# GpSimd takes low weight parts of the mixer's projections, plain float32 leaves, and both ends of the kernel are rearranged

## The chip, the cores and the metric

The kernel runs on one NeuronCore of a Trainium2 chip. TensorE (PE) multiplies matrices, VectorE (DVE), ScalarE (ACT) and GpSimd (POOL) work element by element, SyncE (SP) issues most transfers. The metric is the device time of one execution in microseconds (us). Before the change it is 904.86 us, the median of 3 runs (904.58 to 906.59).

## The reference

The reference is an encoder trunk of two layers on 256 tokens of width 1024, in float32. Each layer adds a mixer and a convolutional feed-forward block to x:

```
h = RMSNorm(x)
p = h @ w_in                       # 1024 -> 16 + 26 * 256 columns
x = x + (sig(gate_dn) * (DeltaNet(q, k, v, beta, g) @ w_dn)
       + sig(gate_hg) * (HGRN2(hq, hf, hb, hi) @ w_hg)) @ w_out
gate, up = RMSNorm(x) @ w_up       # 1024 -> 2 * 2816
x = x + (silu(conv3(gate)) * up) @ w_down
```

Both recurrences run in both directions. q, k and v go through a convolution over 5 tokens and silu; the outputs of the recurrences are normed per head and multiplied with silu(z) or silu(hgate). After two layers comes a final RMSNorm.

## The kernel before, in words

x lies transposed: features on the partitions, the 256 tokens along the free dimension, in four tiles of two feature blocks each (x0 to x3). A product of the input with 256 columns of weights is a projection. The 26 of them in `w_in` have numbers: 0 and 1 are q, 2 and 3 k, 4 and 5 v, 6 to 9 hq, hf, hb, hi of the first head pair, 10 to 13 those of the second, 14 and 15 z, 16 and 17 hgate, 18 to 25 the gates of the branches. The weights of a projection come in two pieces of 128x1024 (four row blocks of 256 columns), 512 KB each.

A projection is computed in one of two ways. `Gemm` (from L221) splits: ScalarE rounds a piece to the type fp32r (wh, L217), VectorE subtracts this from the piece (wl, L218), and TensorE sums three products, wh by the input's high part, wh by its low part, and wl by its high part. In the trace these stand under L149, three records for each row block and half, 48 for a projection. `gemm32` (L262) takes the piece as it is and multiplies in plain float32, without a split; each product leaves two records, 32 for a projection. `OPT["f32"]` names the projections that go that way: 1, 4, 5, 6 and 14 in both layers. 0 to 8, 10 to 12 and the gates have weights as the stationary operand; 9, 13 and 14 to 17 have the tokens there (`tokens=True`). The raw pieces have three buffers, as have wh and wl; SP's queue issues a piece's transfer (L202) when its buffer is free.

Projections 2 and 3 (k) are begun ahead (`Pre`, L356) on x that is not normed yet, in plain float32; the scale of the norm comes from `Rms` (L283): squares on ScalarE, their sum over the feature blocks on VectorE (L300), a product with a column of ones on TensorE (ss, eight records), a square root and a reciprocal (L311, L312). For layer 0 these first matmuls stand at the very start of the kernel, behind the first transfers: SP's queue brings x0, half of the first weight piece, x1, x2, the other half, x3; ScalarE's queue the small vectors `vec`, the constants and a row of scalars.

A mixer's stages are named in `OPT["order"]`: q0, q1, k0, k1, v0, v1 are the convolutions, gs, ks, qs, vt, de and gn, gp small statistics and gram matrices, so the solve of the triangular systems (31 steps on VectorE between transfers through HBM), in the inverse, dl the delta rule, hg the HGRN2 scans, do and ho the output norms, g0 to g7 the gates, br the branch products (pbr), pr the output projection. The program is written in that order; the number behind a name is a priority, by which a planner that simulates the engines' time lines moves a stage's instructions forward on each engine's queue. On its engine every instruction runs in the planned order. A piece's split has a priority of its own (`ahead`).

GpSimd does little: it clears the borders of the convolutions' padded tiles (L517, L518, L1023, L1024) and of the solve's tiles (L664, L665), and copies the masks (L428).

At the end, projection c = 3 of `w_down` in layer 1 (`ffn`, L1007) sums its last six row blocks half by half: first all products of half m = 0, then those of m = 1, both halves in one PSUM bank. Behind it come x's last part (L1057), its squares, their sum, the statistics, and the transposes of x to tokens (`turn`, L1135, sixteen in all) with the final scale (L1147, L1149).

Of the kernel before, what the change touches and what calls it, by code (L numbers as in the profile page):

```python
# [28 lines left out]
    "f32": ((1, 4, 5, 6, 14), (1, 4, 5, 6, 14)),  # L29
# [21 lines left out]
    "x0": (0, 4, 1, 2, 5, 3),  # L51
# [6 lines left out]
    "as": 32,  # L58
    "at": ((32, 40), (56, 40)),
# [59 lines left out]
def trunk(ctx: ExitStack, tc: tile.TileContext, x_in, consts, masks, vec, rows, w16, w_in, w_br, w_out, w_up, w_down, out):  # L119
# [61 lines left out]
    act.dma_start(row.rearrange("p a b -> p (a b)"), rows.broadcast_to([P, DEPTH * 16]))  # L181
    ident = cst[:, C_ID:C_ID + P]
    upper = cst[:, C_U:C_U + P]
    lower = cst[:, C_L:C_L + P]
    pool.memset(ones, 1.0)
# [19 lines left out]
    def split_piece(src, n):  # L205
        with tc.high_priority(offset=OPT["ahead"]):
            return split_piece_(src, n)

    def split_piece_(src, n, pool=None, bufs=0):
# [8 lines left out]
        dve.tensor_tensor(wl[:, :n], raw[:, :n], wh.bitcast(F32)[:, :n], ALU.subtract)  # L218
# [40 lines left out]
    def gemm(src, xh, xl, nk=KT, tokens=False, tail=0, parts=None):  # L259
        return Gemm(src, xh, xl, nk, tokens, tail, parts).run()  # L260
# [876 lines left out]
    for c in range(3):  # L1137
        turn(c)
# [91 lines left out]
```

## Time and profile before

| | |
|---|---|
| median of 3 runs | 904.86 us |
| the profiled execution | 904.76 us |
| its span, first to last instruction | 902.6 us |
| TensorE's mean granted clock | 0.996 |
| busy: PE, DVE, ACT, POOL | 881.7, 670.3, 559.9, 14.0 us |
| TensorE matmul records | 7438 |
| HBM read | 146.75 MB, 165 GB/s over the span |
| a weight piece of 512 KB, issue to landing (median) | 3.4 to 4.2 us |

The profile is one execution, recorded instruction by instruction. Busy time is the union of an engine's instructions. A matmul's record is longer than its step, since matmuls are pipelined; the step between records is read from rows that merge many of them. In the chain of waits each piece has its start, its length and what it was; the chain goes back from the last instruction through what released each one. The views by stretch give the busy time of each engine in a stretch (with the number of instructions in brackets), the granted TensorE clock, the mean busy share of the DMA engines and what they moved. The layers' mixers run from about 26 to 249 us and from 474 to 691 us, the feed-forward blocks from there to 459 us and to 894 us.

### The profile page before, as it was taken

What the parts mean: (1) busy time and instruction counts of PE and PEld (TensorE: products, weight loads), DVE (VectorE), ACT (ScalarE), POOL (GpSimd) and SP (SyncE); (2) the same over time, 40 slices, a digit from 0 to 9 for tenths busy, and PEclk for the clock granted to TensorE, in tenths of its full rate; (3) what the DMA queues carried; (4) which work ended last, traced back from release to release, by engine and by line L of the source; (5) the groups of instructions that cost most, each with busy time, mean ns of one, the idle gap of its engine ahead of it and who ended that gap; (6) DMA issues with size and microseconds to landing.
All of it is one profiled execution on the core that took longest, in us unless ns stands there. A gap on an engine that the chain in (4) does not pass through costs nothing.

```text
span 902.6 us, 18703 instructions
## 1 busy us (share of the span) xinstructions
PE 881.7 (98%) x7438; PEld 862.7 (96%) x7438; DVE 670.3 (74%) x1279; ACT 559.9 (62%) x972; POOL 14.0 (2%) x123
## 2 busy tenths in 40 slices
PE   6999999999999999999999999999999999999997
PEld 5988999999999999999989899999999999999996
DVE  4758898656777988865437889986567898888543
ACT  4698766579466665554427857475764765566443
POOL 0000000000000000000000000000000000000000
PEclk9999999999999999999999999999999999999999
DMA  6455555225557666655514474542356666666562
GB/s 204 141 188 158 193 172 141 64 75 170 184 195 270 208 195 198 192 180 182 164 39 141 164 233 150 177 119 71 95 166 207 188 192 201 192 193 195 182 192 82
DMA packets 51111, 150.07 MB, mean 166 GB/s; under 512 B 13488, under 2 KB 14032, under 8 KB 50768
## 3 DMA queue, kind: packets, MB, share of 16 engines
q1 hardware_dynamic: 50304, 147.96, 51.9%
q8 instruction: 58, 0.95, 0.4%
q10 hardware_dynamic: 720, 0.92, 0.3%
q14 instruction: 29, 0.24, 0.1%
HBM read 146.75 MB, written 2.11 MB: 165 GB/s over the span
## 4 chain that ended last, share of the span: by engine, by line
PE 85%; ACT 5%; DMA 5%; DVE 3%; issue 1%; SPq 0%; DVEq 0%; ACTq 0%
PE ps L149 69%; PE pbr L149 5%; PE pa L857 3%; DMA raw<-in_w_in_dram 3%; DVE wl L218 1%; ACT wh L217 1%; PE po L149 1%; DMA ld<-dg 1%; PE poh L149 1%; PE psb L149 1%; ACT cacc L527 1%; PE pz L693 0%; PE pr L716 0%; DVE cacc L534 0%; PE pz L712 0%
## 5 line engine op out<-in xcount | busy, mean ns | idle before, releaser
L217 ACT CAST wh<-raw 128x1024 fp32r<-128x1024 f32 x244 | 252.7, 1039 | 230.8 <-PE ps L149 132.5
L218 DVE TENSOR_TENSOR wl<-raw,wh 128x1024 fp32r<-128x1024 f32 x244 | 293.7, 1205 | 114.1 <-ACT wh L217 110.8
L149 PE MATMUL ps<-xh,wl 128*128 128x256 f32 x1152 | 320.0, 279 | 1.5 <-DVE wl L218 1.5
L149 PE MATMUL ps<-xh,wh 128*128 128x256 f32 x1152 | 320.4, 279 | 1.0 <-ACT wh L217 1.0
L149 PE MATMUL ps<-xl,wh 128*128 128x256 f32 x1152 | 319.1, 278 | 0.0
L149 PEld LDWEIGHTS ps<-xh,wl 128*128 128x128 f32 x1152 | 215.9, 188 | 2.3 <-DVE wl L218 2.1
L149 PEld LDWEIGHTS ps<-xh,wh 128*128 128x128 f32 x1152 | 216.0, 188 | 1.4 <-ACT wh L217 1.1
L149 PEld LDWEIGHTS ps<-xl,wh 128*128 128x128 f32 x1152 | 216.0, 188 | 0.1
L149 PE MATMUL ps<-hl,wh 128*128 128x256 f32 x352 | 98.0, 279 | 0.0
L149 PE MATMUL ps<-hh,wl 128*128 128x256 f32 x352 | 98.0, 279 | 0.0
L149 PE MATMUL ps<-hh,wh 128*128 128x256 f32 x352 | 97.7, 278 | 0.0
L149 PEld LDWEIGHTS ps<-hl,wh 128*128 128x128 f32 x352 | 66.3, 188 | 0.1
L149 PEld LDWEIGHTS ps<-hh,wl 128*128 128x128 f32 x352 | 66.3, 188 | 0.1
L149 PEld LDWEIGHTS ps<-hh,wh 128*128 128x128 f32 x352 | 66.1, 188 | 0.0
L149 PE MATMUL ps<-xnt,raw 128*128 128x256 f32 x256 | 58.9, 381 | 0.5 <-ACT srk L573 0.5
L149 PEld LDWEIGHTS ps<-xnt,raw 128*128 128x128 f32 x256 | 47.0, 190 | 6.5 <-ACT srk L573 0.7
L149 PE MATMUL ps<-wl,xh 128*128 128x256 f32 x160 | 46.7, 292 | 0.7 <-DVE wl L218 0.7
L149 PE MATMUL ps<-wh,xh 128*128 128x256 f32 x160 | 46.2, 290 | 0.2 <-ACT wh L217 0.2
L149 PE MATMUL ps<-wh,xl 128*128 128x256 f32 x160 | 45.6, 285 | 0.0
L1032 DVE SCALAR_TENSOR_TENSOR cv<-fpad,vecs,cv 128x256 f32<-128x256 f32 x88 | 42.1, 482 | 4.0
L149 PE MATMUL pbr<-ohl,wh 128*128 128x256 f32 x256 | 44.3, 278 | 0.0
L149 PEld LDWEIGHTS pbr<-ohl,wh 128*128 128x128 f32 x256 | 38.5, 189 | 0.0
(279 smaller groups left out, 1440.9 us busy)
## 6 DMA issues: line engine op xcount, KB each, us to landing
raw<-in_w_in_dram SPq DMA_DIRECT2D x99, 512.0 KB, 3.7
raw<-in_w_up_dram SPq DMA_DIRECT2D x88, 512.0 KB, 4.1
raw<-in_w_down_dram SPq DMA_DIRECT2D x40, 512.0 KB, 3.7
raw<-in_w_br_dram SPq DMA_DIRECT2D x16, 512.0 KB, 3.6
raw<-in_w_out_dram SPq DMA_DIRECT2D x16, 512.0 KB, 4.2
cb<-cd SPq DMA_DIRECT2D x2, 1024.0 KB, 5.2
early<-in_w_in_dram SPq DMA_DIRECT2D x4, 512.0 KB, 6.8
raw<-in_w_down_dram SPq DMA_DIRECT2D x8, 256.0 KB, 3.4
```

The lines of the kernel that those rows point to most:

```text
L149: self.prev = chain(pe.matmul(o, lhsT, rhs, start=self.i == 0, stop=self.i == self.n - 1), self.prev)
L217: act.copy(wh[:, :n], raw[:, :n])
L218: dve.tensor_tensor(wl[:, :n], raw[:, :n], wh.bitcast(F32)[:, :n], ALU.subtract)
L527: act.activation(ac_[:, m * T:(m + 1) * T], pad[:, m, 0:T], AF.Identity, scale=w[:, 0:1])
L857: pe.matmul(pa[:, u // 2, u % 2], kc[:, u * P:(u + 1) * P], view(qa[:, 0, u * P:u * P + 1], [[2 * h, 64 // h], [512 + h, 2], [1, h]]), sta ...
L1032: dve.scalar_tensor_tensor(cv, pad[:, i:i + T], w[:, i:i + 1], cv, op0=ALU.mult, op1=ALU.add)
```

## The change

- No projection is left in plain float32: the list `f32` is empty. Projections 1, 4, 5, 6 and 14 of both layers go the split way.
- GpSimd computes the low part wl of projections 1, 4, 5, 14 in layer 0 and 1, 4, 5, 6, 11, 14, 16, 25 in layer 1, twelve in all (`gp`). VectorE computes it for the rest, layer 0's projection 6 among them. The high part stays with ScalarE.
- Ten products of a tile of ones with itself are put on TensorE's queue ahead of everything (`idle`). The memset of the ones comes first on GpSimd's list.
- x's four parts go on SP's queue alone; the first weight piece, in two halves, and the second piece go on ScalarE's queue, ahead of the constants, and `vec` comes last there.
- In the last projection the two halves have PSUM banks and accumulation groups of their own. Between them stand on TensorE the twelve transposes of x0 to x2 (`most`) and the statistics of the sum so far; behind the second half only the last part's squares are added, straight from ScalarE's output.
- The stage orders of both layers and their priorities are others.

```diff
-    "f32": ((1, 4, 5, 6, 14), (1, 4, 5, 6, 14)),
+    "f32": ((), ()),
+    "gp": ((1, 4, 5, 14), (1, 4, 5, 6, 11, 14, 16, 25)),
+    "idle": 10,
-        "k0-2000 k1 gs-9000 ks-2000 de-9000 gn-1000 so-5000 q0-9000 v0 q1-5000 v1-300 vt-9000 hi0-2000 "
-        "hq0-2000 hf0-2000 hb0-2000 gp-3000 qs-3000 hg0-4000 in-9000 z0-3000 dl-3000 hq1 z1-9000 hi1-9000 "
+        "k0-2000 k1 gs-3000 ks-2000 de gn-1000 so-5000 q0-9000 v0 q1-5000 hi0-2000 v1-300 vt-9000 hq0-2000 "
+        "hf0-2000 hb0-5000 gp-3000 qs-3000 hg0-4000 hq1 in-9000 z0-3000 hi1-9000 z1-1000 g0-7000 hb1-300 "
...
+    pool.memset(ones, 1.0)
     pool.memset(epst, EPS)
...
+    early = pm.tile([P, P], F32, tag="d", name="idle", bufs=OPT["d"])
+    idle = None
+    for i in range(OPT["idle"]):
+        idle = chain(pe.matmul(early, ones, ones, start=True, stop=True), idle)
...
-    for item in OPT["x0"]:
-        if item < 4:
-            sp.dma_start(xt[item], x_in[item])
-        else:
-            s = slice(512 * (item - 4), 512 * (item - 3))
-            sp.dma_start(raw0[:, s], w_in[0, 2, 0][:, s])
-    act.dma_start(vecs, vec)
+    raw1 = wp.tile([P, 1024], F32, tag="raw", name="raw", bufs=OPT["raw"])
+    for i in range(4):
+        sp.dma_start(xt[i], x_in[i])
+        if i < 2:
+            s = slice(512 * i, 512 * i + 512)
+            act.dma_start(raw0[:, s], w_in[0, 2, 0][:, s])
+        elif i == 2:
+            act.dma_start(raw1, w_in[0, 2, 1])
...
         act.copy(wh[:, :n], raw[:, :n])
-        dve.tensor_tensor(wl[:, :n], raw[:, :n], wh.bitcast(F32)[:, :n], ALU.subtract)
+        (eng or dve).tensor_tensor(wl[:, :n], raw[:, :n], wh.bitcast(F32)[:, :n], ALU.subtract)
...
+            if mid:
+
+                self.o[1] = pg.tile([P, 512], F32, tag="g", name="ps", bufs=OPT["g"])[:, 0:256]
+                self.gs[1] = Group(nk * 3)
...
+                    if last and self.mid and m and k == self.k:
+                        self.prev = self.mid(self.prev)
...
+        def tail_add(self, sq, after=None):
+            for b in range(2):
+                self.g.mm(self.ps[:, b:b + 1], sq[:, b * P:(b + 1) * P], ones[:, 0:1], after)
...
-                return gemm(src, xh, xl, tokens=tokens, parts=pre.parts.get(c))
+                return gemm(src, xh, xl, tokens=tokens, parts=pre.parts.get(c), eng=pool if c in OPT["gp"][l] else None)
...
+    def most(prev):
+
+        with tc.high_priority(offset=OPT["rp"]):
+            act.activation(spare, final[0].sa[:, 0, 0:1], AF.Sqrt)
+            pts.extend(pm.tile([P, 4, P], F32, tag="dh"[i % 2], name="pt", bufs=OPT["dh"[i % 2]]) for i in range(4))
+            for c in range(3):
+                prev = turn(c, prev)
+            final[0].tail_start(prev)
+            return final[0].g.prev
```

## Rows read from the trace of the kernel before

**Rows 1.** The page: busy us (share of the span) and instructions of each engine.
```profile
PE 881.7 (98%) x7438; PEld 862.7 (96%) x7438; DVE 670.3 (74%) x1279; ACT 559.9 (62%) x972; POOL 14.0 (2%) x123
```
**Rows 2.** The chain of waits in order of time: start us, length us, what.
```profile
16.69 8.63 PE ps L149 x40
...
106.38 2.83 PE ps L149 x24
...
191.67 3.57 PE po L149 x32
...
209.82 7.96 PE ps L149 x70
217.99 5.30 PE ps L149 x45
225.41 5.18 PE pbr L149 x44
...
720.98 142.29 PE ps L149 x1254
```
**Rows 3.** Stretches: length, busy us of each engine, PE clock, DMA share, GB/s.
```profile
0.00:6.02 6.02, 0.00 (x0) 0.03 (x1) 0.62 (x2) 2.12 (x3) 0.58 (x10) 1.00 0.66 194
6.02:11.65 5.63, 5.63 (x13) 4.51 (x14) 3.61 (x9) 1.99 (x4) 0.00 (x0) 1.00 0.98 356
11.65:14.05 2.40, 2.40 (x12) 2.09 (x11) 0.14 (x1) 0.00 (x0) 0.04 (x1) 1.00 0.66 191
25.33:47.00 21.67, 21.67 (x141) 20.22 (x141) 13.93 (x50) 14.35 (x24) 0.41 (x6) 1.00 0.42 132
47.00:82.00 35.00, 32.33 (x208) 29.37 (x208) 26.96 (x70) 31.43 (x71) 1.95 (x3) 1.00 0.52 177
104.00:140.00 36.00, 36.00 (x312) 36.00 (x311) 34.74 (x82) 21.39 (x27) 0.00 (x0) 1.00 0.53 168
500.00:590.00 90.00, 88.07 (x686) 85.35 (x685) 82.24 (x191) 61.67 (x123) 2.90 (x4) 1.00 0.58 179
893.60:902.60 9.00, 2.37 (x20) 1.89 (x18) 3.09 (x7) 3.07 (x7) 0.00 (x0) 0.81 0.31 117
```
**Rows 4.** Groups by form: line, engine, operation, count | busy us, mean ns | idle.
```profile
L217 ACT CAST wh<-raw 128x1024 fp32r<-128x1024 f32 x236 | 247.7, 1053 | 216.2 <-PE ps L149 120.6 <-ACT cv L1030 24.7 <-DMA raw<-in_w_in_dram 24.7
L218 DVE TENSOR_TENSOR wl<-raw,wh 128x1024 fp32r<-128x1024 f32 x236 | 288.1, 1223 | 105.2 <-ACT wh L217 101.9 <-PE ps L149 2.3
L428 POOL CAST mks<-mkf 128x896 uint8<-128x896 f32 x1 | 0.9, 931 | 12.9 <-DMA mkf<-in_masks_dram 12.9
L665 POOL MEMSET ti<- 128x1024 f32 x2 | 1.9, 954 | 39.1 <-DVE np__260 L630 20.9 <-DVE np__5723 L630 18.3
```
**Rows 5.** The page's DMA issues: transfers, KB each, median us to landing.
```profile
raw<-in_w_in_dram SPq DMA_DIRECT2D x99, 512.0 KB, 3.7
```
**Rows 6.** The timeline of the start: start us, length us, instruction, idle before.
```profile
4.92 0.63 ACT L292 ACTIVATE sa<-x 128x512 f32<-128x512 f32 x1 [2.25 <-DMA x<-in_x_dram]
6.02 8.19 PE L149 MATMUL ps<-xw,raw 128*128 128x256 f32 x24 [6.02 <-DMA raw<-in_w_in_dram]
10.34 0.63 ACT L299 ACTIVATE sq<-x 128x512 f32<-128x512 f32 x1 [1.74 <-DMA x<-in_x_dram]
14.05 0.95 PE L149 MATMUL ss<-ones,sa 128*128 128x1 f32 x8
```
**Rows 7.** The end: the timeline's transposes, then the chain's last pieces.
```profile
893.60 0.82 PE L1135 MATMUL pt<-cst,x 128*128 128x128 f32 x6
...
893.80 0.43 DVE x L1057
...
894.71 0.44 DVE sa L300
...
895.19 1.07 PE ss L149 x8
```
**Rows 8.** Waits on GpSimd's queue: who for whom, us, times, longest.
```profile
POOL pad L517 <- PE ps L149: 91.4, 2, 49.4
```

More of the change, by code (lines that the diff above doesn't have):

```diff
@@ L184, in trunk @@
     lower = cst[:, C_L:C_L + P]
-    pool.memset(ones, 1.0)
     def placed(pool, dtype, shape, shift, **kw):
@@ L203, in piece, with split_piece, split_piece_ @@
         return raw
-    def split_piece(src, n):
+    def split_piece(src, n, eng=None):
         with tc.high_priority(offset=OPT["ahead"]):
-            return split_piece_(src, n)
-    def split_piece_(src, n, pool=None, bufs=0):
+            return split_piece_(src, n, eng=eng)
+    def split_piece_(src, n, pool=None, bufs=0, eng=None):
         raw = piece(src, n)
@@ L238, in run @@
                     kn = min(4, end - k0)
-                    wh, wl = self.parts[k0 // 4] if self.parts else split_piece(self.src(k0 // 4), kn * 256)
+                    wh, wl = self.parts[k0 // 4] if self.parts else split_piece(self.src(k0 // 4), kn * 256, self.eng)
                     w += [(wh[:, kk], wl[:, kk]) for kk in range(kn)]
@@ L300, in add, with tail_start, tail_end @@
                     dve.tensor_tensor(self.sa[:, s], self.sa[:, s], sq[:, s], ALU.add)
+        def tail_start(self, after):
+            self.ps = pm.tile([P, 2], F32, tag="d", name="ss", bufs=OPT["d"])
+            self.g = Group(8)
+            for i in range(2):
+                self.tail_add(self.sa[:, i], after)
+        def tail_add(self, sq, after=None):
+            for b in range(2):
+                self.g.mm(self.ps[:, b:b + 1], sq[:, b * P:(b + 1) * P], ones[:, 0:1], after)
+        def tail_end(self):
+            rt = xp.tile([P, 2], F32, tag="rt", name="rt", bufs=2)
+            act.activation(rt, self.ps, AF.Sqrt, bias=epst, scale=1.0 / D)
+            dve.reciprocal(rt, rt)
+            return rt
         def per_token(self, after=None):
@@ L368, in __init__ @@
             self.parts, self.stack = {}, None
-            self.last = None
+            self.last = None if l else idle
         def ahead(self, l):
@@ L1005, in mixer, with ffn @@
         return nxt
-    def ffn(l, rs, xs, first):
+    def ffn(l, rs, xs, first, mid):
         V = vecs[:, l]
@@ L1051, in ffn @@
                 gm = Gemm(lambda i: w_down[l, c, i] if i < 5 else w_down[l, c, i][:, 0:512], hh, hl, NF,
-                          tail=OPT["mt"] if c == 3 else 0)
-                ps = gm.run()
-                parts = 2 if c == 3 and OPT["mt"] else 1
-                for i in range(0, 2, 2 // parts):
-                    s = slice(i, i + 2 // parts)
-                    dve.tensor_tensor(xx2[c][:, s], xx2[c][:, s], ps.rearrange("p (a b) -> p a b", a=2)[:, s], ALU.add)
+                          tail=OPT["mt"] if c == 3 else 0, mid=mid if c == 3 else None)
+                if last and c == 3:
+                    final.append(rs)
+                gm.run()
+                parts = 2 if gm.tail else 1
+                if gm.tail:
+                    for i in range(2):
+                        dve.tensor_tensor(xx2[c][:, i], xx2[c][:, i], gm.o[i], ALU.add)
+                else:
+                    dve.tensor_tensor(xx2[c], xx2[c], gm.ps.rearrange("p (a b) -> p a b", a=2), ALU.add)
                 if not last:
                     pre.add(c)
-                rs.add(c, parts)
+                if last and c == 3:
+                    with tc.high_priority(offset=OPT["rp"]):
+                        sq = tmp("sq").rearrange("p (a b) -> p a b", a=2)
+                        for i in range(2):
+                            act.activation(sq[:, i], xx2[c][:, i], AF.Square)
+                            rs.tail_add(sq[:, i], gm.prev)
+                else:
+                    rs.add(c, parts)
                 if last:
@@ L1065, in ffn @@
                 if OPT["pc"]:
-                    pre.last = gm.g.prev
+                    pre.last = gm.prev
                 rest = todo[OPT["ek"]:] + [(j, k) for j in range(len(PRE)) for k in (6, 7)]
@@ L1079, in meet @@
         return rs, rm
-    first = [raw0]
-    pre = Pre(0, lambda src: first.pop() if first else piece(src, 1024))
+    first = [raw0, raw1]
+    pre = Pre(0, lambda src: first.pop(0) if first else piece(src, 1024))
     rs = Rms()
@@ L1121, in trunk, with turn @@
         dve.tensor_scalar(oms[:, l], omlb[:, l], 128.0 ** -0.5, None, op0=ALU.mult)
-    for l in range(OPT["layers"]):
-        nxt = mixer(l, pre, rs)
-        pre, rs = ffn(l, *nxt)
-    op = ctx.enter_context(tc.tile_pool(name="op", bufs=4, reuse_waits="tile"))
-    pts = [pm.tile([P, 4, P], F32, tag="dh"[i % 2], name="pt", bufs=OPT["dh"[i % 2]]) for i in range(4)]
-    prev = None
-    def turn(c):
-        nonlocal prev
+    pts, final = [], []
+    def turn(c, prev):
         for b in range(2):
@@ L1135, in turn @@
                 prev = chain(pe.transpose(pts[2 * (c // 2) + b][:, k % 4], x[k][:, b * P:(b + 1) * P], ident), prev)
-    for c in range(3):
-        turn(c)
-    rt = rs.per_token(prev)
-    prev = rs.last
-    turn(3)
+        return prev
+    def most(prev):
+        with tc.high_priority(offset=OPT["rp"]):
+            act.activation(spare, final[0].sa[:, 0, 0:1], AF.Sqrt)
[4 more added lines that the diff above has]
+            return final[0].g.prev
+    for l in range(OPT["layers"]):
+        nxt = mixer(l, pre, rs)
+        pre, rs = ffn(l, *nxt, most if l == OPT["layers"] - 1 else None)
+    op = ctx.enter_context(tc.tile_pool(name="op", bufs=4, reuse_waits="tile"))
+    rt = rs.tail_end()
+    turn(3, rs.g.prev)
     for i in range(4):
```

27 lines of the change are left out of this document (14 added, 13 removed), and 12 rows, old and new, of the table OPT.

## The prediction

> **What bounds the kernel now.** I read the page's busy shares first: TensorE is busy 98% of the span, VectorE 74%, ScalarE 62%, GpSimd 2% [rows 1]. A busy TensorE is not one at its peak, so I looked at its pace next. In the chain of waits the matmuls of one kind follow each other at an even step: 0.2158 us for a record of plain float32 (40 in 8.63 us), 0.1135 us for a record of the split kind (1254 in 142.29 us), 0.118 us where the tokens are the stationary side (24 in 2.83 us) [rows 2]. So TensorE is not only occupied, it streams; almost the whole time is the sum of its matmuls. Then I read the stretches for holes: within the mixers TensorE is idle 2.67 us in 47 to 82 us and 1.93 us in 500 to 590 us; the largest holes are the 6.02 us before its first matmul and 6.63 us of the last 9.0 us [rows 3]. ScalarE is nearly full at 47 to 82 us (31.43 of 35) and VectorE at 104 to 140 us (34.74 of 36) and 500 to 590 us (82.24 of 90) [rows 3]. These are the places where work put on another engine could open a hole.
>
> **Plain float32 becomes split: the main term.** A projection has 16 pairs of a 128-row and a 256-column product. In plain float32 each leaves two records, 32 in all, 32 x 0.2158 = 6.90 us. Split, it is three products, 48 records. Eight of the ten have weights stationary: 48 x 0.1135 = 5.45 us, 1.45 us less each, 11.6 us together. The two z projections have tokens stationary: 48 x 0.118 = 5.66 us, 1.24 us less each, 2.5 us together. Sum: -14.1 us, all of it on the engine that sets the time. By the bounds: nothing, if the new splits are late by as much (below), and no more than 14.1, since the records are counted.
>
> **What the split asks of the other engines.** Each projection has two pieces of 128x1024. ScalarE gets 10 x 2 casts of 1.053 us, 21.1 us [rows 4]. The subtractions go to GpSimd for 12 projections (24 pieces); VectorE, at 1.223 us each [rows 4], gains two pieces in layer 0 (hq0) and loses six in layer 1 (hf1, z2, g7), -4.9 us in all. What a subtraction costs on GpSimd the trace does not show. The nearest rows are its cast of 128x896, 0.931 us, that is 1.06 us for 1024 elements with one input, and a memset of 128x1024 of 0.954 us [rows 4]. Lower bound 1.06 us; with a second input read in turn 2.1 us; upper bound twice that, 4.2 us. I take 2.1, as it is the cast's row for each input. The Trainium skill, "GPSIMD Engine Reference", section "Elementwise — side-by-side cycle accounting", has 4497 ns for a two-input add of 2048 float32; by it 1024 would be about 2.25 us, an estimate from that page, and the sum would be the same.
>
> Is 2.1 us hidden? A piece holds one of three raw buffers for its DMA (3.7 us) [rows 5], its cast and its subtraction: 3.7 + 1.05 + 2.1 = 6.9 us, a third of it 2.3 us, and TensorE takes 24 x 0.1135 = 2.72 us per piece. So the ring keeps ahead, until the subtraction takes over 3.4 us. I count it at nothing; TensorE's own matmuls of the piece before are the cover.
>
> **ScalarE in layer 0's first part.** From 25.33 to 82 us ScalarE is busy 14.35 + 31.43 = 45.8 us of 56.7 [rows 3]. Four of the former float32 projections lie here (q1, v0, v1, hq0): eight casts more make 54.2 us, and TensorE's own part shrinks by 4 x 1.45 to 50.9 us. 3.3 us too much, if nothing else is brought forward. TensorE may take later projections instead, which need 2.1 us of ScalarE for 5.45 us of its own. I take +1.5 us; bounds 0 and 3.3. What falls late in exchange is the chain conv, k statistics, decay, gram, solve. Between the delta rule's output matmuls (to 195.2 us) and the branch matmuls from 225.41 us there are long runs of other projections, 7.96 and 5.30 us the longest two [rows 2]; a chain late by up to these 13.3 us can be passed by moving them forward.
>
> **Stage order.** It can at most take away the 2.67 and 1.93 us of idle time, and could as well add as much; I take 0, bounds -4.6 and +4.6.
>
> **The start.** The first part of x lands at 4.92 us, TensorE starts at 6.02 us when its weights have landed, and 24 records take 8.03 us until the statistics start at 14.05 us [rows 6]; at 0.2158 us each it would be 5.18. In 6.02 to 11.65 us it ran 13 of them, 433 ns apart, the step of the lower level of its clock (1.2 GHz), in 11.65 to 14.05 us the rest at the step of 2.4 GHz [rows 3]; the granted clock's column reads 1.00 in both, so I go by the step. The clock rose after 5.6 us of matmuls. The ten added products read a tile of ones that a memset, now placed first, fills within about the first us. Each is two records of half the columns, by the same rows about 0.215 us at the lower level, so 4.3 us together, over at about 5.4 us: just when the first weights, now the first transfer of ScalarE's queue instead of the second of SP's, can have landed. Of the 2.85 us of slow pace I take most as saved (the clock may still be low for a while), and 0.6 us for starting earlier, if x keeps up. Its last part lands at 10.34 us today [rows 6]. In the first 6.02 us the DMAs moved 194 GB/s, 1.17 MB, then 356 GB/s [rows 3]. x is 1.05 MB on SP's queue; with as much from ScalarE's beside it 2.1 MB are to be moved, which at these rates is done at 8.6 to 9.1 us (at 307 GB/s, the mean of 6.02 to 14.05 us). The square of 0.63 us [rows 6] and the sum behind it bring the statistics to about 10.5, and the records before them end at about 11: 3 us before 14.05. SP's queue then goes on with the masks and weights; the small vectors, last on ScalarE's, land at about 11.7 us by 2.9 MB at 307 GB/s and are needed at about 13: cover of 1 us. Together I take -2.6 us; bounds +0.5 (weights or vectors late) and -3.5.
>
> **The last pair.** Today the last matmul ends at 893.78 us; then VectorE's add 0.43, ScalarE's square as long, VectorE's sum 0.44 and eight records of statistics 1.07 us [rows 7]. With the halves in banks of their own the first half's add and square run beside the second half's 18 matmuls, the sum is gone, and four records remain behind: 0.48 + 0.5 = -1.0 us. But the six transposes that today run in the shadow behind the last matmul (0.82 us) [rows 7] and eight records of statistics (0.9 us) now stand ahead of the second half on TensorE: +1.5. Net +0.5 us; bounds -1.0 and +1.5.
>
> **The sum.** 902.6 - 14.1 + 1.5 - 2.6 + 0.5 = 887.9 us of span. The profiled execution took 904.76 us, 2.16 us more than its span; with that 890 us. That execution is 0.1 us from the median of the runs, 904.86, so nothing has to be scaled.
>
> **Rivals.** *GpSimd and VectorE get in each other's way* (about 900 us). The trace has no GpSimd instruction with two inputs, and its one cast stands in the start where VectorE is nearly idle [rows 3], so nothing in the rows excludes it. If a subtraction on GpSimd holds off VectorE's two-input work for its 2.1 us, then in 500 to 590 us, where four of the projections (eight pieces) lie, VectorE needs 82.2 + 16.8 - 2.4 = 96.6 us where TensorE's part is now 84.3: 12 us over, with 3 us more for z0 at layer 0's full stretch. Since VectorE also has work with PSUM inputs and the gates can be moved, I give two thirds, 10 us. The Trainium skill, "SBUF — State Buffer", section "Who interferes with whom", states just that: a VectorE instruction with two SBUF inputs and a GpSimd one that reads SBUF exclude each other for a whole instruction. For it speaks VectorE's mix (the subtraction itself has two SBUF inputs); against it, that over the span VectorE has a quarter of its time free [rows 1].
>
> *GpSimd's own queue* (about 898 us). The padding memsets of the convolutions wait there for buffers, 91.4 us in two waits [rows 8]; a subtraction queued behind one waits as long, and TensorE behind it. Or the subtraction takes 4.2 us: the ring's step is then 9.0 / 3 = 3.0 us, 0.26 us over for 24 pieces, 6 us, and with one blocked piece in each layer about 8. Against it: the order on the queue follows planned times, in which that wait is known.
>
> *ScalarE becomes the bound* (about 910 us, slower). If every one of the 21.1 us of casts pushes the chain to the solve, since it runs there with 3.6 us to spare in 35 [rows 3], then 21.1 - 14.1 - 2.6 + 0.5 = +4.9 us. It decides from the point where the chain is later than the 13.3 us of projections that can be put in its place. Against it: over the span ScalarE has 38% of its time free [rows 1], and half of the casts are in layer 1, where 500 to 590 us shows 61.67 of 90 [rows 3].
>
> **How the numbers follow.** The forecast has 64%, the shared engines 18%, GpSimd's queue 8%, ScalarE 10%. The forecast's own range is 884 to 896. For eight times in ten: below, 890 less the 4.6 us of order, 0.9 of the start and 1.5 each of the end and ScalarE give 881.5; I take 882. Above, the range takes in the two rivals near 900 and ends at 902. About 0.2%, 1.8 us, is what a measurement can tell from no change. Faster is the forecast and most of the cases near 900: 0.86; within the bound 0.04; slower 0.10.
>
> **What would show it.** Right: no plain float32 records on the projections' normed input; 480 split records in their place at 0.114 to 0.118 us; the first 24 records of weights in 5.2 to 6 us; statistics near 11 us; GpSimd's subtraction near 2.1 us; TensorE idle within the mixers under 8 us. Wrong: TensorE waiting on GpSimd's low parts by more than some us; VectorE's two-input instructions longer or with gaps beside GpSimd's; the branch matmuls starting no earlier than the removed records allow; holes around 50 to 80 us that end on ScalarE's casts.

## The result: 3% slower

The changed kernel takes 932.16 us, the median of 4 runs (927.35 to 934.76), against 905.7 us (904.58 to 906.59, 4 runs) for the kernel before beside it: a ratio of 1.0298, 95% interval 1.0268 to 1.0327. The forecast was 890 us in a range of 882 to 902; the time lies outside, on the other side. The profiled execution took 934.76 us with a span of 932.9.

First the page of the changed kernel: busy time and instructions of each engine, GpSimd's subtraction, and VectorE's convolution step.

```profile
PE 890.0 (95%) x7626; PEld 874.4 (94%) x7626; DVE 700.2 (75%) x1273; ACT 578.0 (62%) x992; POOL 76.4 (8%) x147
...
L225 POOL TENSOR_TENSOR wl<-raw,wh 128x1024 fp32r<-128x1024 f32 x24 | 62.5, 2610 | 213.3 <-ACT wh L224 166.1
...
L565 DVE SCALAR_TENSOR_TENSOR cacc<-pad,vecs,cacc 128x256 f32<-128x256 f32 x72 | 42.7, 638 | 0.1
```

TensorE has less to stream and is busy for longer than before [rows 1]; the convolution step's mean is 638 ns, 476 ns before. The pages' chain of waits, followed back from the last instruction, says on which engine the end hangs (shares of the span, before and after):

```profile
PE 85%; ACT 5%; DMA 5%; DVE 3%; issue 1%; SPq 0%; DVEq 0%; ACTq 0%
```
```profile
PE 71%; DVE 13%; ACT 9%; DMA 3%; issue 3%; POOL 0%; DVEq 0%; ACTq 0%; SPq 0%; POOLq 0%
```

VectorE's part of the chain rose from 3 to 13%, TensorE's fell from 85 to 71% (e15 below, as fast as the kernel before, has 6 and 80%). Next the stretches, first of the kernel before, then of the changed one: layer 0's mixer (from its statistics to its last branch product), layer 0's feed-forward block, the same two of layer 1. Columns as in [rows 3].

```profile
14.10:249.10 235.00, 229.73 (x1906) 221.69 (x1905) 175.56 (x396) 168.28 (x319) 4.15 (x11) 1.00 0.47 148
249.10:459.40 210.30, 210.30 (x1812) 209.15 (x1811) 155.48 (x246) 115.56 (x166) 2.92 (x45) 1.00 0.61 194
459.40:690.70 231.30, 228.33 (x1898) 220.43 (x1898) 179.15 (x388) 151.72 (x305) 3.47 (x13) 0.99 0.45 141
690.70:893.80 203.10, 203.10 (x1789) 203.10 (x1788) 152.69 (x234) 117.21 (x170) 2.81 (x44) 1.00 0.59 183
```
```profile
10.60:256.40 245.80, 229.76 (x1985) 223.78 (x1986) 189.76 (x398) 174.40 (x327) 25.05 (x19) 0.98 0.46 143
256.40:475.00 218.60, 214.59 (x1812) 213.21 (x1811) 159.84 (x246) 118.07 (x169) 10.05 (x49) 1.00 0.60 192
475.00:720.50 245.50, 230.25 (x1979) 223.31 (x1980) 190.94 (x382) 162.74 (x316) 37.88 (x25) 0.97 0.42 129
720.50:924.90 204.40, 204.40 (x1801) 204.40 (x1800) 153.23 (x235) 116.25 (x171) 2.81 (x44) 1.00 0.59 182
```

By place, the 30.3 us of span are: start -3.5, mixer 0 +10.8, feed-forward 0 +8.3, mixer 1 +14.2, feed-forward 1 +1.3, end -0.8. So most of the loss is in the mixers, where the ten projections lie (feed-forward 0 is taken up below: 3.9 us at its end, most of the rest goes with a slower pace). There TensorE's idle time (length less busy) grew from 5.3 to 16.0 us and from 3.0 to 15.3 us. And its busy time did not shrink, though each mixer's records are worth some 7 us less at the steps of [rows 2]: part of them ran at half pace. In the changed kernel's mixers the granted clock fell to 0.5, its lower level of 1.2 GHz, six times, five times for 3.4 us and once for twice that; the kernel before has one such stretch of 3.4 us there, at 462.2 us. Two of these stretches of the changed kernel, below the six us ahead of each:

```profile
29.70:35.70 6.00, 3.82 (x34) 3.62 (x33) 5.07 (x12) 1.71 (x3) 2.86 (x4) 1.00 0.56 176
531.40:537.40 6.00, 3.13 (x20) 2.40 (x20) 5.21 (x14) 5.97 (x13) 0.00 (x0) 1.00 0.02 7
```
```profile
537.40:540.80 3.40, 3.28 (x15) 3.28 (x16) 3.37 (x7) 3.37 (x5) 1.73 (x1) 0.50 0.53 155
35.70:39.10 3.40, 3.40 (x16) 3.40 (x17) 0.00 (x0) 3.37 (x7) 2.31 (x1) 0.50 0.10 12
```

TensorE had been busy for 3.82 and 3.13 of the six us before. Seven times 3.4 us at half pace, against once, are about 10 us more of TensorE's time (six times half of 3.4, an estimate); how much of it reaches the end is not shown.

What GpSimd does to VectorE is seen in the timeline. VectorE's and GpSimd's instructions of the changed kernel from 26 us on (start us, length us):

```profile
26.21 0.16 DVE L1163 TENSOR_SCALAR oms<-omlb 128x8 f32<-128x8 f32 x1
...
26.96 2.37 DVE L1162 TENSOR_SCALAR omlb<-lb 128x8 f32<-128x8 f32 x1
```
```profile
26.67 2.63 POOL L225 TENSOR_TENSOR wl<-raw,wh 128x1024 fp32r<-128x1024 f32 x1
```

An instruction of 0.16 us takes 2.37 us beside a subtraction: it ends when that ends. This does not happen to each. Beside the next subtraction the second of two convolution steps keeps its 0.47 us, and the short instruction behind it is held:

```profile
29.25 0.87 DVE L565 SCALAR_TENSOR_TENSOR cacc<-pad,vecs,cacc 128x256 f32<-128x256 f32 x2
30.04 2.34 DVE L1163 TENSOR_SCALAR oms<-omlb 128x8 f32<-128x8 f32 x1
```
```profile
29.55 2.80 POOL L225 TENSOR_TENSOR wl<-raw,wh 128x1024 fp32r<-128x1024 f32 x1 [0.24 <-ACT wh L224]
```

Both held instructions stand in the chain of waits:

```profile
27.04 2.29 DVE omlb L1162
30.04 2.34 DVE oms L1163
```

Set against the median of their form before, 20 of VectorE's instructions beside the 24 subtractions took 39 us more in all; some 30 others beside them took no longer than before. The Trainium skill, "SBUF — State Buffer", section "Who interferes with whom", has GpSimd and VectorE block each other for a whole instruction where VectorE's has two SBUF inputs or runs in a two-port mode. The trace agrees on the length of the block; which of the two the short instructions here were, it does not show. Once the block stands in the open, at the layers' boundary (the chain of the changed kernel, then who TensorE waited for):

```profile
470.18 4.49 DVE xw L415 x2
475.05 1.07 PE ss L150 x8
```
```profile
PE ss L150 <- DVE sa L314: 3.9, 1, 3.9
```

Two subtractions for the next mixer lie beside the two short scalings (0.35 us each before), and TensorE waits 3.9 us for the sum behind them.

### The profile page after: what moved, and what is told of

Read it like the earlier page. It is cut to its first block, busy times and chain, and to the rows that moved or that the text cites. A ratio compares the mean times of both kernels' runs of the same rounds, so it can differ in the third digit from the quotient of the medians.

```text
span 932.9 us, 19153 instructions
## 1 busy us (share of the span) xinstructions
PE 890.0 (95%) x7626; PEld 874.4 (94%) x7626; DVE 700.2 (75%) x1273; ACT 578.0 (62%) x992; POOL 76.4 (8%) x147
## 4 chain that ended last, share of the span: by engine, by line
PE 71%; DVE 13%; ACT 9%; DMA 3%; issue 3%; POOL 0%; DVEq 0%; ACTq 0%; SPq 0%; POOLq 0%
PE ps L150 59%; PE pbr L150 4%; DVE cacc L565 3%; DVE wl L225 2%; ACT wh L224 2%; PE pa L888 2%; DMA raw<-in_w_up_dram 1%; DMA xd<-xx 1%; DVE pr L685 1%; DVE qa L899 1%; PE po L150 1%; DVE xs L687 1%; DMA ti<-xd 1%; ACT cacc L558 1%; PE poh L150 1%
## 5 line engine op out<-in xcount | busy, mean ns | idle before, releaser
L224 ACT CAST wh<-raw 128x1024 fp32r<-128x1024 f32 (+1 forms) x264 | 273.1, 1037 | 218.9 <-PE ps L150 120.1
L150 PE MATMUL ps<-xh,wh 128*128 128x256 f32 x1280 | 361.4, 283 | 5.7 <-ACT wh L224 3.4
L150 PE MATMUL ps<-xh,wl 128*128 128x256 f32 x1280 | 360.3, 283 | 5.7 <-DVE wl L225 3.4
L150 PE MATMUL ps<-xl,wh 128*128 128x256 f32 x1280 | 358.7, 281 | 0.0
L150 PEld LDWEIGHTS ps<-xh,wl 128*128 128x128 f32 x1280 | 244.1, 191 | 7.4 <-DVE wl L225 4.6
L150 PEld LDWEIGHTS ps<-xh,wh 128*128 128x128 f32 x1280 | 243.1, 190 | 7.2 <-ACT wh L224 4.2
L150 PEld LDWEIGHTS ps<-xl,wh 128*128 128x128 f32 x1280 | 243.1, 190 | 0.1
L225 POOL TENSOR_TENSOR wl<-raw,wh 128x1024 fp32r<-128x1024 f32 x24 | 62.5, 2610 | 213.3 <-ACT wh L224 166.1
L150 PE MATMUL ps<-wh,xh 128*128 128x256 f32 x192 | 54.6, 285 | 0.6 <-ACT wh L224 0.6
L565 DVE SCALAR_TENSOR_TENSOR cacc<-pad,vecs,cacc 128x256 f32<-128x256 f32 x72 | 42.7, 638 | 0.1
```

Source lines behind the costliest of these rows:

```text
L150: self.prev = chain(pe.matmul(o, lhsT, rhs, start=self.i == 0, stop=self.i == self.n - 1), self.prev)
L224: act.copy(wh[:, :n], raw[:, :n])
L225: (eng or dve).tensor_tensor(wl[:, :n], raw[:, :n], wh.bitcast(F32)[:, :n], ALU.subtract)
L565: dve.scalar_tensor_tensor(a, pad[:, m, j:j + T], w, a, op0=ALU.mult, op1=ALU.add)
```

## The experiments

Medians in us; where runs stood beside different runs of the kernel before, the ratios to those count. The planner gives each program an order of its own. Only e8 (that of e1) and e15 and e19 (that of before) keep another's order; every other difference between two runs can hold the order besides the edit. "Old order" and "new order" below mean the list of stages alone. Mixer lengths are of the profiled executions.

**What each part does.** Four kernels beside each other (before: 904.56), then one more.

e1: only the start and the end of the change; the ten in plain float32, VectorE for every subtraction, the old order.
```diff
-    "f32": ((), ()),
+    "f32": ((1, 4, 5, 6, 14), (1, 4, 5, 6, 14)),
...
-    "gp": ((1, 4, 5, 14), (1, 4, 5, 6, 11, 14, 16, 25)),
+    "gp": ((), ()),
...
```


> The changed kernel with the projections left as before (ten in plain float32, no GpSimd subtraction) and the stage order of before: only the first transfers, the ten early products and the last pair are changed. Shared port, stage order and split theories all expect the same here: the start gives back 3.5 us (statistics at 10.6 us instead of 14.1, as in the changed kernel's trace), the end 0.8 us, so about 901 us. If it comes out at 905 or more, the gain of the start is lost again later in layer 0.

e2: the same with `f32` empty, so split on ScalarE and VectorE.

> The changed kernel with the stage order of before and every low part on VectorE: the ten projections are split, GpSimd has no subtraction. Shared port theory (each GpSimd subtraction holds VectorE off for 2.1 us): no holding off, but VectorE has 20 more pieces of 1.22 us (24 us), some of which is exposed: 888 to 898 us. Stage order theory: as the order is the old one, about 888 us. Split theory (the casts on ScalarE and the subtractions, wherever they run, fill the mixers): about 925 to 935 us, as slow as the changed kernel.

e3: split, with GpSimd's list, old order.

> The changed kernel with nothing but the stage order of before put back; GpSimd has its 24 subtractions. Shared port theory: VectorE still loses about 39 us beside them, 920 to 935 us. Stage order theory: 888 to 895 us. Split theory: 925 to 935 us.

e4: the changed kernel with `gp` empty.

> The changed kernel with the 24 subtractions of GpSimd on VectorE instead, stage order as changed. Shared port theory: VectorE gets 24 x 1.22 = 29 us of work and loses 39 us of being held off, and nothing of it sits at the layer boundary any more (3.9 us there): 890 to 905 us. Stage order theory: 925 to 935 us, as the order stays. Split theory: 930 us or more, since VectorE has more to do.

e9: e1 with the new order.

> The changed kernel with its new stage order, but with the ten projections in plain float32 as before and no subtraction on GpSimd. Theory (the split is what costs; the order is a matter of some us): 905 to 912, as with the old order, 909. Rival (a stage order fits one program, and its priorities are worth tens of us): over 918, and the loss in the mixers.

| ratio to before (95%) | old order | new order |
|---|---|---|
| ten in plain float32 | e1 1.0047 (1.0025 to 1.0068) | e9 1.0139 (1.0102 to 1.0176) |
| split, VectorE subtracts | e2 1.0444 (1.0401 to 1.0487) | e4 1.042 (1.038 to 1.046) |
| split, GpSimd subtracts | e3 1.0343 (1.0296 to 1.039) | changed 1.0298 (1.0268 to 1.0327) |

The times are 909.29, 945.82, 935.78 and 942.86 us for e1 to e4, 916.33 for e9. So the split costs 36 us, more than any theory had for e2; GpSimd gives 10 of them back with either list of stages, despite what it does to VectorE, and the new order costs plain float32 some 8 us and gives the split some 3. The start and the end, alone in e1, cost 4 us instead of gaining any.

**Is it TensorE's sum?** Three kernels take the split apart, in the old order with the ends of e1; they were run beside before at 906.16.

e5: the ten with the casts alone.
```diff
+        wh = wp.tile([P, 1024], F32R, tag="wh", name="wh", bufs=OPT["w"])
+        act.copy(wh[:, :n], raw[:, :n])
+        v = wh[:, :n].rearrange("p (k c) -> p k c", c=256)
+        return v, v
```


> As e2 (stage order of before, no GpSimd), but the ten projections leave the low part out: ScalarE casts each piece, nothing is subtracted, and the third product reads the high part again, so TensorE has the same 48 records. VectorE theory (the 20 subtractions fall on VectorE where it is full, the 62 steps of the solve wait in line behind them, and what follows the solve is late): 895 to 910 us. ScalarE theory (the 20 casts are what is too much): about 940 us, like e2's 946.

e6b: the ten with the subtractions alone.
```diff
+            dve.tensor_tensor(wl, raw, stand.bitcast(F32).rearrange("p k c -> p (k c)"), ALU.subtract)
+        return stand, wl.rearrange("p (k c) -> p k c", c=256)
```


> As e2, but no casts for the ten projections: TensorE multiplies with the input's high part in place of the weights' high part, VectorE subtracts it from the piece for the low part (20 subtractions of 1.22 us), so the weights' high parts are left out. VectorE theory: 930 to 945 us, like e2. ScalarE theory: 890 to 900 us.

e6: with neither (ScalarE casts a quarter of each piece).
```diff
+            act.copy(wh[:, :256], raw[:, :256])
+            w = [wh[:, :256]] + [stand[:, k] for k in range(1, 4)]
```


> As e2, but the ten projections ask next to nothing of the other engines: ScalarE casts a quarter of each piece (0.4 us), and for the other three quarters TensorE multiplies with the input's own high part in place of the weights, so the weights are left out; 48 records as in e2. Both theories: the term of the prediction by itself, 14 us less TensorE than e1, 888 to 898 us. If TensorE's split records are themselves the trouble (their order, their pace): 930 us or more.

e10: e6 with twelve more records per projection.
```diff
+            self.fill = 12 if parts and isinstance(parts[0][0], Blocks) else 0
...
+            for i in range(self.fill):
+                wh = w[i % 4][0]
...
+                    self.g.mm(self.o[i % 2], wh[:, 0:P], self.xh[i % 8])
```


> The run with neither cast nor subtraction (e6, 924.9), with twelve more split records on each of the ten projections, so that each takes TensorE 6.8 us again, as in plain float32. It leaves out what e6 left out. Theory (a projection's length on TensorE is what the other engines need to keep up; it was cover, not cost): the 14 us put back change nothing or shorten the time, 909 to 925. Rival (the kernel is the sum of TensorE's work and the loss of e6 comes on top, from the order or the buffers): 935 to 940.

Measured: e5 932.08 (ratio 1.0277), e6b 942.23 (1.0412), e6 924.91 (1.0207, interval 1.0171 to 1.0243), e10 921.1 (1.0195, 1.0163 to 1.0227). Even with next to nothing asked of ScalarE and VectorE the split is some 15 us behind e1, and 14 us of records put on TensorE lengthen nothing in sum. But the two layers answer differently (mixers, us, from the statistics to the last branch product):

| | layer 0 | layer 1 |
|---|---|---|
| before | 235.0 | 231.3 |
| e1, plain float32 | 237.6 | 234.0 |
| e6, split, neither | 235.0 | 252.6 |
| e10, e6 and twelve records each | 242.2 | 242.8 |
| e5, casts | 242.4 | 252.9 |
| e6b, subtractions | 250.6 | 253.2 |
| e2, both | 245.7 | 257.7 |

The mixers of e6, then of e10:

```profile
10.80:245.80 235.00, 226.06 (x1985) 221.62 (x1986) 174.44 (x396) 170.12 (x328) 4.25 (x11) 0.99 0.47 150
456.00:708.60 252.60, 231.16 (x1977) 225.26 (x1978) 178.33 (x388) 159.78 (x316) 3.48 (x13) 0.96 0.40 126
```
```profile
11.20:253.40 242.20, 233.04 (x2046) 229.47 (x2046) 175.01 (x396) 167.14 (x326) 4.30 (x11) 0.99 0.45 145
463.70:706.50 242.80, 232.66 (x2038) 228.05 (x2038) 178.50 (x389) 157.17 (x315) 3.47 (x13) 0.99 0.42 132
```

In layer 0 the 61 added records keep TensorE busy for 7.0 us more, and the mixer is 7.2 us longer: there, without casts and subtractions, TensorE's sum seems to count. In layer 1 TensorE is busy for 1.5 us longer and idle for 11.3 us less, the clock's mean is 0.99 instead of 0.96, and the mixer is 9.8 us shorter. There TensorE's sum is not what sets the time. The traces have VectorE's instructions in another order in e10 than in e6, so that the added records themselves did this is not shown. Casts or subtractions alone cost something over e6 in layer 0 (7.4 and 15.6 us), and hardly in layer 1 (0.3 and 0.6). What TensorE waits for in e6's layer 1, from 495 to 530 and from 530 to 575 us:

```profile
PE ps L151 <- ACT iv L877: 5.7, 1, 5.7
PE ps L151 <- ACT sn L868: 2.1, 1, 2.1
```
```profile
PE pa L907 <- DVE qa L918: 4.1, 1, 4.1
PE ps L151 <- DVE wl L226: 1.5, 1, 1.5
```

The longest of these holes end on ScalarE (its reads of an accumulator, which free it) and VectorE (the scans); 1.5 us of them are for a weight's low part.

**What GpSimd costs VectorE.** e8: e1 with 20 subtractions on GpSimd that nobody reads, one for each piece of the ten. The planned order on TensorE, VectorE and ScalarE is that of e1, instruction by instruction.
```diff
+            junk = wp.tile([P, 1024], F32R, tag="wl", name="junk", bufs=OPT["w"])
+            with tc.high_priority(offset=OPT["ahead"]):
+                pool.tensor_tensor(junk, raw, raw, ALU.subtract)
```


> As e1 (ten projections in plain float32, stage order of before), and for each of their 20 pieces GpSimd subtracts the piece from itself into a tile that nobody reads: 2.4 us of GpSimd each, no work for the other engines. Shared port theory (each one holds VectorE off for 2.1 us, and what VectorE is late by sets the end): 925 to 940 us. If VectorE's holding off is covered: 909 us, as e1.

924.34 us (1.0188, 1.0154 to 1.0222): 15 us over e1's median, 13 by the ratios, for work that no one waits for. Layer 0's mixer of e1, then of e8:

```profile
10.60:248.20 237.60, 230.30 (x1906) 221.88 (x1905) 175.76 (x396) 168.37 (x319) 4.24 (x11) 1.00 0.46 149
```
```profile
11.00:259.00 248.00, 234.50 (x1905) 225.36 (x1904) 187.29 (x396) 168.00 (x318) 23.56 (x21) 0.97 0.46 142
```

The same 396 instructions keep VectorE busy for 11.5 us more, and the mixer is 10.4 us longer; layer 1's is 6.0 us longer (240.0 against 234.0).

**Is it the work between the solve's steps?** In layer 1 the solve's 31 steps (62 instructions) take 51.3 us before, 64.5 in the changed kernel and 78.4 in e2: VectorE's order has 117, 131 and 163 instructions between the first and the last. e13 (the changed kernel) and e14 (e1) put the HGRN2 scans behind the last step.
```diff
+            def scan(e):
+                with tc.issue_after(solved[-1].ins):
+                    hgrn(e)
...
-                stages[f"hg{e}"] = lambda e=e: hgrn(e)
+                stages[f"hg{e}"] = lambda e=e: scan(e)
```


> The changed kernel with one rule more: on VectorE the instructions of the HGRN2 scans (qa, kb, tt, at) stand behind the last step of the same layer's solve. Planned between the first and last of the 62 steps are then 72 and 87 instructions (107 and 131 in the changed kernel). Theory (the chain through the solve is what came late, since VectorE is full there and other work stands between its steps): the solve of layer 1 takes 40 to 50 us instead of 64, the branch products start 8 us or more earlier, 910 to 924. Rival (VectorE's sum is what counts, the order of its work isn't): what is moved back comes due later, 928 to 945.

> The same rule in the kernel with the ten projections in plain float32, the old stage order and the new ends (909). Theory: here the chain has cover, so little is to be had, 903 to 912, and the rule closes most of the gap between the two kernels. Rival: the scans come late and the branches wait for them, over 915.

952.19 (1.0542, 1.0499 to 1.0584) and 919.13 us (1.0186, 1.0136 to 1.0235): my theory falls. In e13 layer 1's solve took 39.9 us and its inverse began at 604.7 instead of 627.9 us, but the scans' last product came at 702.3 instead of 681.3 and the branches ended at 737.4 instead of 720.3. TensorE now waits for the scans (470 to 750 us of e13):

```profile
PE pa L878 <- DVE ksum L872: 7.6, 1, 7.6
```

The branches need both chains, both run through VectorE, and to let one pass delayed the other.

**Is it VectorE's load?** e11 (e1) and e12 (e3) compute the convolutions over two taps.
```diff
-                for j in range(2, 5):
+                for j in range(2, 2):
```


> The kernel with the ten projections in plain float32, old stage order and new ends (e1, 909.3), with the mixers' convolutions over two taps instead of five: left out are the 36 multiply-adds of 128x256 in each layer that VectorE does for the other three taps, about 17 us of VectorE a layer. It is the reference point for the next run. Both theories: faster than 909, by 5 to 25, since the chain to the solve gets shorter.

> The same convolutions over two taps (the same 36 multiply-adds a layer left out) with the ten projections split and GpSimd's subtractions, old stage order and new ends (e3, 935.8, which was 26.5 over e1). Theory (the split is slow because VectorE has no room for what it asks, in the stretch up to the solve's end): with 17 us of VectorE free in each layer the distance to the plain float32 run beside it falls to 13 us or less. Rival (it is slow for another reason: the planned order, TensorE's clock, ScalarE's casts): the distance stays at 20 to 30 us.

925.09 (1.0227, 1.0197 to 1.0257) and 926.03 us (1.0227, 1.0187 to 1.0266). The distance is gone, from 26.5 to 1 us, as the theory wanted, but only 10 us of it because the split got faster: plain float32 with 34 us less for VectorE got 16 us slower, which no theory had expected. Layer 1's mixer of e11:

```profile
463.10:710.70 247.60, 234.20 (x1898) 223.29 (x1898) 166.58 (x352) 162.25 (x313) 3.47 (x13) 0.97 0.43 132
```

VectorE works 12.6 us less there than before, TensorE has the same records, and the mixer takes 16.3 us more (13.6 more than e1's). What changed besides is the order that the planner made. With e9 (the same work, another order: +8 us) this suggests, without showing it, that the order by itself can be worth ten us and more. The pair is thus no clean test of VectorE's load.

**Which of the ten?** e17 leaves 1, 4, 5 in plain float32, e18 leaves 6 and 14 instead; VectorE subtracts. The edit of e17:
```diff
-    "f32": ((), ()),
+    "f32": ((1, 4, 5), (1, 4, 5)),
```


> Only z0 and hq0 (projections 14 and 6) of both layers are split, casts on ScalarE and subtractions on VectorE; the convolutions' three (1, 4, 5) stay in plain float32; old order, new ends. All ten split that way made 945.8, none 909.3. If the cost goes by the number of projections, 4 of 10: 924. Theory (the cost sits where VectorE and ScalarE are full before the solve, with the convolutions): 909 to 917. Rival (z0 and hq0 were the cover that TensorE needs while the solve runs): over 925.

> The counterpart: projections 1, 4 and 5 of both layers are split, casts on ScalarE and subtractions on VectorE, while 6 and 14 stay in plain float32; old order, new ends. By number, 6 of 10: 931. Theory (the cost sits with the convolutions): 935 to 946. Rival (z0 and hq0 were the cover): under 925.

916.68 (1.0136, 1.0099 to 1.0172) and 929.48 us (1.0282, 1.0244 to 1.0321): 7 and 20 us over e1, 28 of the 36 together. Per projection it is 1.9 and 3.4 us: none comes free. e18 stays under its theory and lies nearer to the count by number. And that the cost sits with the convolutions' projections holds in layer 1 alone: there e17's mixer is 2.1 us longer than e1's and e18's 20.4; in layer 0 it is 6.8 and 3.0 us.

**The old order by force.** e15 is the kernel before with the ten early products alone; its order is that of before. e19 is e15 with the ten split, GpSimd subtracting, and every engine held to that order.
```diff
+        for i, j in zip(row_, row_[1:]):
...
+                chain(engine.made[j][0], engine.made[i][1])
```


> The kernel before with one edit: the ten products of ones ahead of everything, and the memset of ones first on GpSimd's list. First transfers, end, stage order and plain float32 as before; the planned order on all engines is that of the kernel before. If the start counts by itself: the statistics begin 2 to 3 us earlier and the time falls by as much, 902 to 903. If the start's gain is taken back by waits for weights in layer 0, as in e1 (3.5 us at the statistics, 0.9 left at the end of layer 0's mixer): 904 to 905.

> e15 with the ten projections split, their casts on ScalarE, their subtractions on GpSimd (20 pieces, no others), and the orders of the kernel before held by force: VectorE runs the same instructions in the same order, ScalarE too with the 20 casts put in between, and on TensorE the three split products stand where the plain float32 product stood. Theory (most of the loss is the other order that the planner makes of the split): held to the old order it costs at most what GpSimd's hold-off costs with equal orders, 15 us (e8 against e1), less what TensorE saves: 902 to 918. Rival (the casts and the subtractions come late wherever they are queued, and the order only follows from that): as with the free order, 925 to 945.

905.64 (1.0018, 0.9994 to 1.0042: no difference, though its statistics begin 1.1 us earlier, at 12.98 us) and 943.92 us (1.0428, 1.0401 to 1.0456): that theory falls too. The old order does not save the split; the planner's own order for it came out 8 us faster (e3, with the ends of the change and more subtractions on GpSimd). But since both run the same lists, they show where the time goes. Stretches of e15: from 25 us to the solve's first step, the solve, and from there to the last branch product; then the same of e19:

```profile
25.00:92.70 67.70, 65.12 (x416) 59.73 (x416) 45.85 (x125) 56.14 (x125) 3.30 (x10) 1.00 0.53 168
92.70:138.40 45.70, 45.23 (x387) 44.87 (x386) 43.34 (x108) 28.23 (x36) 0.00 (x0) 1.00 0.55 175
138.40:248.10 109.70, 108.42 (x1047) 107.11 (x1046) 76.32 (x140) 76.41 (x145) 0.00 (x0) 1.00 0.41 126
```
```profile
25.00:113.80 88.80, 70.33 (x511) 67.58 (x511) 57.34 (x125) 63.90 (x134) 26.79 (x19) 0.88 0.45 137
113.80:158.60 44.80, 42.56 (x365) 42.16 (x364) 43.60 (x109) 28.79 (x37) 0.96 (x1) 1.00 0.50 162
158.60:269.10 110.50, 109.17 (x1054) 107.86 (x1053) 76.51 (x140) 77.30 (x145) 0.00 (x0) 1.00 0.40 125
```

All 21 us of layer 0 are lost before the solve begins: the 125 instructions of VectorE take 11.5 us more beside GpSimd, ScalarE has 7.8 us more of its own, and TensorE is idle for 18.5 us instead of 2.6. In e15 all records of the five plain projections lie ahead of the solve's first step. So behind it both kernels have the same work, and take the same time: the lateness is neither caught up nor added to. Layer 1 repeats it: 25.1 us behind at its statistics, 36.7 at the solve's first step, 39.9 at the end. VectorE's list shows the steps, each beginning beside a subtraction (e19's chain of waits; these take 0.17 us in e15):

```profile
46.08 2.42 DVE ac L204
48.73 2.42 DVE ac L204
51.17 2.30 DVE ac L204
```

By 74 us VectorE is 11.9 us late; a low part of VectorE's that waits 10.7 us for ScalarE's cast brings it to 24, of which 3 come back. That last wait is the forced order's own, so 21 us is an upper bound for what the split itself costs layer 0 in this order.

## Why the prediction was wrong

**"Sum: -14.1 us, all of it on the engine that sets the time"**: this is the step that failed, together with what the split asks of the other engines, which I put at next to nothing. The records are as predicted (79 or 81 more in each mixer, the 320 of plain float32 gone). But with them the time hangs on TensorE less: its idle time in the two mixers grew by 23.0 us, to 31.3 (my sign of being right was under 8), stretches at half pace took some 10 us of its time, and its part of the chain of waits fell while VectorE's rose. With equal orders (e19 against e15) the split projections cost 21.1 us ahead of layer 0's solve, where TensorE is idle for 18.5 us instead of 2.6. I read the share of 98% as a bound that would hold after the change too. Where the casts and subtractions are left out the term shows in part, in layer 0 alone: e6's mixer is 2.6 us shorter than e1's, of 7 us expected. By my reading of these runs the plain float32 projections were cover: 6.9 us each of matmuls that need nothing of ScalarE or VectorE but their result's evacuation, to stream while the chain from the convolutions to the solve runs through those two.

**"I count it at nothing; TensorE's own matmuls of the piece before are the cover"**: the ring did keep ahead. GpSimd's subtraction took 2.61 us in the mean (2.1 taken; 2.35 the shortest), and TensorE's waits for it are short, 1.3 us at the longest. The Trainium skill, "GPSIMD Engine Reference", section "Elementwise — side-by-side cycle accounting", has 4497 ns for 2048 columns, by which 1024 would take about 2.25 us, an estimate; the shortest in the trace is close to that. What I left out are the others in the same queues: what stands beside the subtractions on VectorE, and what stands behind the casts on ScalarE. For the first, 13 to 15 us are shown with equal orders (e8 against e1). For the second there are 7 us (e5 over e6), with orders that differ.

**"A chain late by up to these 13.3 us can be passed"**: only a little. Counted from each layer's statistics, the changed kernel's solve ends 13.5 and 19.2 us later than before, and its last branch product comes 10.8 and 14.2 us later: 2.7 and 5.0 us were passed. In e19, whose order is held, nothing is: 21.1 us at layer 0's solve, 21.0 at its last branch product.

**The rivals.** The first was right in its mechanism and near in its price (10 us given; 13 to 15 measured in e8), and it bore the wrong sign for the part: without GpSimd the kernel is 10 us slower still (e2, e4). VectorE is not busy for longer there (369.9 us in the two mixers of e2, 379.7 in e3), so that is not its load; that the subtractions do more harm in VectorE's own queue is my reading and not shown. The hold-off came on top of the loss, not in its place. The slower rival, ScalarE, had the right direction and the right point of decision (a chain later than TensorE can cover), but by e5 and e6b over e6 the casts are the smaller part: 7 us against the subtractions' 17, with orders that differ.

**"I take 0, bounds -4.6 and +4.6"** (stage order): too narrow. I read the idle time that an order could remove, and not what it could add. e9 puts some 8 us on the new order where it doesn't fit the work, nearly all of it in layer 1's mixer (243.0 us against e1's 234.0). The changed kernel's order is worth some -3 us to the split.

**The start and the end.** The statistics begin 3.5 us earlier (2.6 predicted, 3.5 the bound), with the early products over at 5.39 us and 24 records in 5.18 us:

```profile
1.05 4.34 PE idle L166 x20
5.39 5.18 PE ps L150 x24
10.61 1.07 PE ss L150 x8
```

Of these 3.5 us e1 has 0.9 left at the end of layer 0's mixer, up to which VectorE's order is that of before. ScalarE waits for weights for 3.5 us more instead: its casts from the statistics to 145 us, before and in e1:

```profile
ACT wh L217 <- DMA raw<-in_w_in_dram: 10.9, 6, 3.6
```
```profile
ACT wh L224 <- DMA raw<-in_w_in_dram: 14.4, 8, 4.6
```

So this gain at the start is for the most part gone at the end. The last pair made the tail behind the last split product 0.8 us shorter and the last feed-forward block 1.3 us longer: +0.5, as predicted. What else e1 lost is in layer 1's mixer, 234.0 us against 231.3, where the planner's order is another.

**What stays open.** Why e6, with nothing added on ScalarE or VectorE but 0.4 us a piece, is some 15 us behind e1. All of it is in layer 1's mixer: there the solve takes 64.9 us instead of 53.9, with 142 of VectorE's instructions in it instead of 119, and ends 19.5 us later from the statistics. The order that e6 gets, the holes and the lower clock behind them go together, and no run here parts them: to hold e6 to e1's order was not tried. So the cause of the changed kernel's loss in layer 1 is shown in part only. Of e19's 39.9 us the forced order's own share isn't known either. None of the versions beats the kernel before; e15 equals it.

## What to carry to other kernels

That an engine is 98% busy does not say that it will set the time when its work takes another form: ask what the new form wants of the other engines, and where. Work that asks nothing of them can be cover for their chains; a cheaper form that asks each of them for a step can lose more there than it saves. To add work to the supposed bound is a test, but one to be read stage by stage and with the order of the instructions held: e10 alone, by its sum, would have misled. GpSimd beside VectorE held up instructions that have nothing to do with it, and here that was still the cheaper place for the subtractions.

## What the runs showed of the hardware

- Beside GpSimd's 24 two-input subtractions 20 of VectorE's instructions, 0.16 to 1.23 us long otherwise, took 1.2 to 2.9 us; some 30 others beside them kept their length. 20 unread subtractions cost a kernel 13 to 15 us, with the order on the other engines unchanged.
- In the changed kernel's mixers TensorE's granted clock went down to 0.5 six times, for 3.4 us and once for 6.8 us. In the six us ahead of these TensorE had been busy for 2.1 to 5.3 us; by then it mostly streamed again (3.40 of 3.40 us busy in four of them), at half the pace.
- Split records have two paces. In the chain, layer 0's up-projection steps at 116.2 ns before (179.91 us for 1548) and 118.8 ns in the changed kernel (176.51 us for 1486); over the block TensorE was busy for 214.59 us instead of 210.30 with as many records. e2 has the slower pace too, e1, e3 and e4 have not. Nothing in the traces tells why.

```profile
279.52 179.91 PE ps L149 x1548
```
```profile
292.89 176.51 PE ps L150 x1486
```
